# A decoder trunk in fp32: gate and up products of the feed-forward stages by seven quarter products in place of eight

## Chip, core and metric

One core of a Trainium2 chip runs the whole kernel in one launch. The metric is the device time of an execution in microseconds; the profile is one execution of its own, recorded by the hardware profiler. PE is TensorE, DVE is VectorE, ACT is ScalarE, POOL is GpSimd, SP is the engine that issues the loads.

## What is computed

Two layers, each a half-step feed-forward stage, a mixing stage of three kinds of token mixers, and a second half-step feed-forward stage; at the end an RMS norm. There are 512 tokens of width 1024, and the feed-forward width is 2816. The change touches the four feed-forward stages alone:

```python
def rms_norm(x, w):
    xf = x.astype(jnp.float32)
    y = xf * lax.rsqrt(jnp.mean(xf * xf, axis=-1, keepdims=True) + NORM_EPS)
    return (y * w.astype(jnp.float32)).astype(x.dtype)

def swiglu_ffn(h, wg, wu, wd):
    return (jax.nn.silu(h @ wg) * (h @ wu)) @ wd

for l in range(DEPTH):
    h = rms_norm(x, ffn1_norm[l])
    x = x + 0.5 * swiglu_ffn(h, ffn1_w_gate[l], ffn1_w_up[l], ffn1_w_down[l])
    ...
    x = x + mixed @ w_out[l]
    h = rms_norm(x, ffn2_norm[l])
    x = x + 0.5 * swiglu_ffn(h, ffn2_w_gate[l], ffn2_w_up[l], ffn2_w_down[l])
return rms_norm(x, final_norm)
```

## The kernel before

Activations lie transposed, features on the 128 partitions and the 512 tokens along the row: x is 8 tiles of 128x512. To hold fp32 accuracy every matrix operand is split into two fp32r tiles, hi (a cast, on ACT) and lo (operand minus hi, on DVE), and a product is three matmuls per 128 rows of depth: hi by xh, hi by xl, lo by xh. `mm3` (L217) issues them.

A feed-forward stage has 22 blocks of 128 features, in GROUPS of 8, 8 and 6. For each block `mm3` makes pg (gate, 24 matmuls of 128 weight columns by 512 tokens) and pu (up, 24 more) in PSUM. `gated` then multiplies pg by rstd (DVE), takes silu (ACT), multiplies by rstd again (POOL, g<-g,rstd), multiplies pu by that (DVE, u), and splits u into ah (ACT) and al (DVE). The norm works this way: the tokens that enter the products, xh and xl, are x times the norm's weight and not yet divided by the root mean square; the row factor rstd is applied to the products. After a group come its down products pd for 8 output blocks, which are added to x on DVE.

A stage starts before rstd is known: `hold` is the number of first blocks whose `gated` waits (2 in the first stage, 1 in the three others). Then `stats_rows` spreads rstd over the partitions (ps_rb, four small matmuls and a copy), and the held blocks are finished.

Weights come by `load`: SP fetches 1 MB (1024 rows by 256 columns, two feature blocks, as 128x8x256) into one of 2 raw buffers. `dense_units` splits each half of it in turn: hi and lo of 128x1024, of which there are W_BUFS = 4 slots each. So a raw buffer is free for the next load when its second half has been cast and subtracted, and a slot is free when the matmuls that read it have ended.

In the second half of the last stage, `end`, tokens are taken 256 at a time, so matmuls there are 256 wide.

The order of instructions on each engine is set by the tile framework's scheduler, which runs a cost model over the program when it is built; the code gives the program order, priorities and the sizes of the pools. Semaphores follow from what each instruction reads and writes.

## Time and profile before

| | |
|---|---|
| three timed runs | 2185.99, 2188.7, 2189.69 us; median 2188.7 |
| the profiled execution's own time | 2192.0 us |
| its span, first to last instruction | 2190.2 us |
| instructions | 31776, of them 13079 matmuls |
| granted clock of TensorE, mean | 0.992 |
| bytes moved | 203.08 MB, mean 93 GB/s |

The span is the time that the profile's rows divide up; about 2 us of the execution lie around it. A row of a group of instructions reads: line and engine, operation, result <- operands by the program's names, partitions x elements of result and operand, number; then busy us and mean ns of one; then the engine's idle time just before them, and what ended most of it. Line L149 is the helper through which DVE, ACT and POOL record every instruction, so groups are told apart by names. A row of the timeline has the start, the length, the engine and the operation, and in brackets the idle time before it and what ended that. A row of the chain has the start and length of a run of instructions that the end waited for.

### The profile page before, as it was taken

Reading aid. Unit: us, or ns where it says so; the run is one execution under the profiler, and the core shown is the slowest. Engines: PE = TensorE matmul, PEld = TensorE weight load, DVE = VectorE, ACT = ScalarE, POOL = GpSimd, SP = SyncE. Lnnn points to the kernel's source line nnn. Section 1 sums busy time; section 2 is a strip of 40 time slices with the busy share of each in tenths; the row PEclk is TensorE's granted clock in tenths of the full one; section 3 lists DMA queues with packets and bytes.
Section 4 is the critical chain, followed back from the end, with each engine's and each line's share of the span. In section 5 each row is a group of like instructions: output and inputs, shape, how many; then the busy total and the mean of one; then the engine's idle time right before and its main releaser. Section 6 shows DMA issues by size and latency. Waiting matters only on the chain.

```text
span 2190.2 us, 31776 instructions
## 1 busy us (share of the span) xinstructions
PE 2154.9 (98%) x13079; PEld 1829.6 (84%) x13079; DVE 1147.9 (52%) x1980; ACT 842.4 (38%) x1319; POOL 500.4 (23%) x466
## 2 busy tenths in 40 slices
PE   8999999998999999999999999999899999999998
PEld 7888888887988788888888888888889888888888
DVE  5544345468497743433543343364866876434335
ACT  5322224555555422222432222254654544222225
POOL 2201013454333210101211010133633412101011
PEclk9999999999999999999999999999999999999999
DMA  4323234221123323232232322242121232323223
GB/s 155 126 78 116 77 106 140 73 78 40 59 60 106 97 97 96 78 115 80 94 116 96 97 97 96 82 148 79 59 59 40 73 103 88 104 94 99 96 87 126
DMA packets 197757, 203.08 MB, mean 93 GB/s; under 512 B 7626, under 2 KB 189292, under 8 KB 197612
## 3 DMA queue, kind: packets, MB, share of 16 engines
q1 hardware_dynamic: 197612, 201.05, 29.0%
q8 instruction: 103, 1.69, 0.3%
q14 instruction: 42, 0.34, 0.0%
HBM read 194.74 MB, written 6.29 MB: 92 GB/s over the span
## 4 chain that ended last, share of the span: by engine, by line
PE 86%; DVE 9%; ACT 2%; issue 1%; POOL 0%; DMA 0%; SPq 0%; DVEq 0%; ACTq 0%; POOLq 0%
PE pd L217 22%; PE pu L217 22%; PE pg L217 22%; PE ps_fm L260 7%; PE ps_tm L260 5%; PE ps_out L260 2%; DVE aw L149 1%; PE ps_scan L265 1%; DVE lo L149 1%; PE ps_ss L265 1%; DVE blk_p L149 1%; DVE x L149 1%; PE ps_ao L265 1%; DVE flo L149 1%; PE ps_al L265 0%
## 5 line engine op out<-in xcount | busy, mean ns | idle before, releaser
L149 ACT CAST hi<-raw 128x1024 fp32r<-128x1024 f32 (+2 forms) x369 | 379.2, 1028 | 1094.2 <-PE pg L217 323.0
L149 DVE TENSOR_TENSOR lo<-raw,hi 128x1024 fp32r<-128x1024 f32 (+2 forms) x325 | 390.2, 1201 | 80.9 <-ACT hi L149 68.5
L149 POOL TENSOR_TENSOR g<-g,rstd 128x512 f32<-128x512 f32 x88 | 150.2, 1706 | 1130.2 <-ACT g L146 1130.2
L217 PE MATMUL pd<-ah,hi 128*128 128x512 f32 (+1 forms) x752 | 282.0, 375 | 0.0
L217 PE MATMUL pd<-ah,lo 128*128 128x512 f32 (+1 forms) x752 | 281.6, 375 | 0.0
L217 PE MATMUL pd<-al,hi 128*128 128x512 f32 (+1 forms) x752 | 281.6, 375 | 0.0
L217 PE MATMUL pg<-xl,hi 128*128 128x512 f32 x704 | 275.0, 391 | 1.0 <-DVE xl L149 1.0
L217 PE MATMUL pu<-xh,hi 128*128 128x512 f32 x704 | 274.4, 390 | 0.6 <-ACT hi L149 0.6
L217 PE MATMUL pg<-xh,hi 128*128 128x512 f32 x704 | 274.5, 390 | 0.1
L217 PE MATMUL pg<-xh,lo 128*128 128x512 f32 x704 | 274.2, 389 | 0.0
L217 PE MATMUL pu<-xh,lo 128*128 128x512 f32 x704 | 274.1, 389 | 0.0
L217 PE MATMUL pu<-xl,hi 128*128 128x512 f32 x704 | 273.9, 389 | 0.0
L149 DVE TENSOR_TENSOR u<-pu,g 128x512 f32<-128x512 f32 x88 | 60.9, 692 | 280.7 <-PE pu L217 265.2
L149 DVE SCALAR_TENSOR_TENSOR x<-pd,x 128x512 f32<-128x512 f32 (+1 forms) x104 | 67.4, 649 | 229.3 <-PE pd L217 229.0
L149 DVE TENSOR_TENSOR g<-pg,rstd 128x512 f32<-128x512 f32 x88 | 60.8, 691 | 206.8 <-PE pg L217 206.7
L217 PEld LDWEIGHTS pd<-al,hi 128*128 128x128 f32 x752 | 141.4, 188 | 25.7
L217 PEld LDWEIGHTS pd<-ah,lo 128*128 128x128 f32 x752 | 141.3, 188 | 25.4
L217 PEld LDWEIGHTS pd<-ah,hi 128*128 128x128 f32 x752 | 141.1, 188 | 25.5
L217 PEld LDWEIGHTS pg<-xl,hi 128*128 128x128 f32 x704 | 132.3, 188 | 29.3 <-DVE xl L149 2.1
L217 PEld LDWEIGHTS pg<-xh,hi 128*128 128x128 f32 x704 | 132.5, 188 | 27.8 <-ACT xh L149 0.4
L217 PEld LDWEIGHTS pu<-xh,hi 128*128 128x128 f32 x704 | 132.1, 188 | 28.2 <-ACT hi L149 1.0
L217 PEld LDWEIGHTS pu<-xh,lo 128*128 128x128 f32 x704 | 132.3, 188 | 27.5
(331 smaller groups left out, 3778.5 us busy)
## 6 DMA issues: line engine op xcount, KB each, us to landing
raw<-in_ffn_w_gate_dram SPq DMA_DIRECT2D x43, 1024.0 KB, 5.1
raw<-in_ffn_w_up_dram SPq DMA_DIRECT2D x43, 1024.0 KB, 5.1
raw<-in_ffn_w_down_dram SPq DMA_DIRECT2D x32, 1024.0 KB, 4.7
raw<-in_w_in_dram SPq DMA_DIRECT2D x20, 1024.0 KB, 5.2
raw<-in_w_in_dram SPq DMA_DIRECT2D x32, 512.0 KB, 3.6
raw<-in_ffn_w_down_dram SPq DMA_DIRECT2D x20, 768.0 KB, 4.4
xd<-x SPq DMA_DIRECT2D x16, 256.0 KB, 2.5
raw<-in_w_out_dram SPq DMA_DIRECT2D x16, 256.0 KB, 2.6
```

Of the source, the lines that this page charges most:

```text
L149: return f(*args, **kw)
L217: self.nc.tensor.matmul(ps, a[:, k, :], b, start=n == 0, stop=n == 3 * nk - 1)
L260: self.nc.tensor.matmul(ps, a, b, start=start, stop=stop)
L265: self.nc.tensor.matmul(ps, a, b, start=start, stop=stop)
```

## The change

The gate and up products of 18 of the 22 blocks of each stage are made in pairs of blocks by a form of Strassen's method. A pair has a weight of 1024 by 256 and 512 tokens of depth 1024. The weight is cut into four quarters of 512x128 (two halves of the depth, two blocks), the tokens into four of 512x256 (two halves of the depth, two halves of the tokens). Eight products of quarters become seven, on sums of weight quarters and sums of token quarters.

- GROUPS become 6, 6, 6 and 4 blocks. The first 4 blocks of each stage (PLAIN) are made as before; the other 18 are 9 pairs: one in the first group, three, three and two in the next.
- `tokens_mixed`, once per stage after rstd is known: 8 normalised tiles xn (DVE, with weight and rstd), 16 sums tmix of 128x256 (8 on POOL, 8 on DVE), and hi and lo (bh, bl) of the four kinds of quarters, 28 tiles. It stands in the code behind the first block that isn't held.
- `quarter_units`: for each pair the raw gate and up weights, 8 sums of quarters ws on POOL (128x512 each), and for each of the seven products a hi and a lo slot, in which gate and up have a half each: two ACT casts and two DVE subtractions of 128x512.
- `quarters`: for each product 12 matmuls of 256 tokens (four depth blocks by three) for gate and 12 for up, accumulated in pq_y, pq_x and pq_z. Three products are read out on the way to ACT copies (snap), and sums of PSUM and snap are made on DVE, then silu, the multiplication and the split of u. Since xn is normalised, there is no multiplication by rstd, on DVE or on POOL.
- The split tokens xh, xl move to the general pool m (66 buffers, before 50), and two pads shift the pools' addresses.

```diff
-GROUPS = ((0, 8), (8, 8), (16, 6))
+GROUPS = ((0, 6), (6, 6), (12, 6), (18, 4))
+PLAIN = 4
+ORDER = (1, 2, 6, 5, 7, 3, 4)
-M_BUFS = 50
+M_BUFS = 66
...
+    def tokens_mixed(self, w):
...
+        for j in range(KD // 2):
+            xa, xb = self.t2("xn"), self.t2("xn")
+            for d, t in ((j, xa), (j + KD // 2, xb)):
+                v.scalar_tensor_tensor(t, self.x[d], w[:, d:d + 1], self.rstd, ALU.mult, ALU.mult)
+            ta, tb = self.t2("tmix"), self.t2("tmix")
+            gp.tensor_tensor(ta[:, a], xa[:, b], xa[:, a], ALU.subtract)
+            gp.tensor_tensor(tb[:, a], xb[:, b], xa[:, b], ALU.subtract)
+            v.tensor_tensor(ta[:, b], xb[:, b], ta[:, a], ALU.subtract)
+            v.tensor_tensor(tb[:, b], xb[:, a], ta[:, b], ALU.subtract)
...
+            for t, ps in ((xb, (2, 3)), (ta, (5, 6)), (tb, (7, 4))):
+                h, l = self.t2("bh", F32R), self.t2("bl", F32R)
+                nc.scalar.copy(h, t)
+                v.tensor_tensor(l, t, h.bitcast(F32), ALU.subtract)
...
+    def quarter_units(self, srcs):
...
+            def summed(p):
+                for q in parts:
+                    t = self.t2("ws").rearrange("p (k f) -> p k f", k=hk)
+                    x, y, op = {5: (q[21], q[4], ALU.add), 6: (q.get(5), q[1], ALU.subtract),
+                                7: (q[1], q[21], ALU.subtract), 3: (q[2], q.get(6), ALU.subtract)}[p]
+                    nc.gpsimd.tensor_tensor(t, x, y, op)
+                    q[p] = t
+            for p in (5, 6, 7, 3):
+                summed(p)
+            for p in ORDER:
...
+                for i, q in enumerate(parts):
+                    h, l = (t[:, i * hk:(i + 1) * hk, :] for t in (hi, lo))
+                    nc.scalar.copy(h, q[p])
+                    nc.vector.tensor_tensor(l, q[p], h.bitcast(F32), ALU.subtract)
...
+    def quarters(self, units, xq):
...
+        for p in ORDER:
+            ws = next(units)
+            for i in range(2):
...
+                for k in range(hk):
+                    xh, xl = xq[p][k]
+                    for w, r in ((wh, xh), (wh, xl), (wl, xh)):
+                        nc.tensor.matmul(ps, w[:, k, :], r, start=m == 0 and p in (1, 2, 5), stop=m == 3 * hk - 1 and p in (2, 3, 4),
+                                         skip_group_check=True)
...
+                if p == 1:
...
+                    nc.scalar.copy(s1[i], ps)
+                elif p == 2:
+                    nc.vector.tensor_tensor(c1[:, a], ps, s1[i], ALU.add)
...
+                elif p == 7:
+                    nc.vector.tensor_tensor(c2[:, b], ps, s5[i], ALU.add)
+                elif p == 3:
+                    nc.vector.tensor_tensor(c1[:, b], ps, s16[i], ALU.add)
...
     def ffn(self, wg, wu, wd, layer, norm, meanwhile=None, begun=None):
...
+            plain = 0 if gi else PLAIN
...
-            for f in range(nf):
+            for f in range(plain):
...
+                if f == hold:
+                    xq = self.tokens_mixed(w)
+            units = self.quarter_units([m[:, (f0 + plain) * P:(f0 + nf) * P] for m in (wg, wu)])
+            for f in range(plain, nf, 2):
+                act += self.quarters(units, xq)
```

What this does to POOL's queue, at the second group of the first stage (g is the gate of a block, the number is the buffer, the brackets name the semaphores that an instruction waits for). Before, one multiplication per block:

```order
L149 TENSOR_TENSOR g_1258<-g_1258,rstd_434 128x512 [waits Activation_49]
L149 TENSOR_TENSOR g_1326<-g_1326,rstd_434 128x512 [waits Activation_49]
L149 TENSOR_TENSOR g_1398<-g_1398,rstd_434 128x512 [waits Activation_49]
L149 TENSOR_TENSOR g_1466<-g_1466,rstd_434 128x512 [waits Activation_49]
L149 TENSOR_TENSOR g_1538<-g_1538,rstd_434 128x512 [waits DMAHW3_49,DMAHW2_49,DMAHW4_49,DMAHW1_49,DMAHW5_49,DMAHW0_49,DMAHW7_49,PE_49,Activation_49]
```

Now, the sums ws of the group's second pair; raw_1511 is its gate and raw_1513 its up:

```order
L154 TENSOR_TENSOR ws_1515<-raw_1511 128x512 [waits DMAHW0_49,PE_49]
L154 TENSOR_TENSOR ws_1517<-raw_1513 128x512 [waits DMAHW1_49,PE_49]
L154 TENSOR_TENSOR ws_1519<-ws_1515,raw_1511 128x512 [waits PE_49,Pool_49]
L154 TENSOR_TENSOR ws_1521<-ws_1517,raw_1513 128x512 [waits DVE_49,Pool_49]
L154 TENSOR_TENSOR ws_1523<-raw_1511 128x512 [waits PE_49]
L154 TENSOR_TENSOR ws_1525<-raw_1513 128x512 [waits PE_49]
L154 TENSOR_TENSOR ws_1527<-raw_1511,ws_1519 128x512 [waits PE_49,Pool_49]
L154 TENSOR_TENSOR ws_1529<-raw_1513,ws_1521 128x512 [waits PE_49,Pool_49]
```

Eight sums for two blocks stand where two multiplications stood, and the first ones wait for the loads of the pair itself.

DVE at the same pair, where before a block had g, u, al and two lo:

```order
L149 TENSOR_TENSOR g_1466<-pg_1408,rstd_434 128x512 [waits PE_49]
L149 TENSOR_TENSOR lo_1550<-raw_1477,hi_1549 128x1024 [waits Activation_49]
L149 TENSOR_TENSOR u_1470<-pu_1437,g_1466 128x512 [waits PE_49,Pool_49]
L149 TENSOR_TENSOR lo_1579<-raw_1508,hi_1578 128x1024 [waits Activation_49]
L149 TENSOR_TENSOR al_1473<-u_1470,ah_1472 128x512 [waits DMAHW6_49,Activation_49]
```

Now, from the end of the first pair (buffers 1238 to 1241 and 1499 to 1504 are its gate, up and split) into the second (lo from 1532 on). Slots 1532, 1568, 1602 and 1634 are those of products 1, 2, 6 and 5:

```order
L154 TENSOR_TENSOR u_1240<-pq_z_1385,snap_1296 128x256 [waits PE_49]
L154 TENSOR_TENSOR u_1240<-u_1240,g_1238 128x512 [waits DVE_49,Activation_49]
L154 TENSOR_TENSOR lo_1532<-raw_1513,hi_1531 128x512 [waits DMAHW1_49,Activation_49]
L154 TENSOR_TENSOR lo_1568<-raw_1513,hi_1567 128x512 [waits Activation_49]
L154 TENSOR_TENSOR al_1500<-u_1240,ah_1499 128x512 [waits Activation_49]
L154 TENSOR_TENSOR u_1241<-pq_y_1283,g_1239 128x256 [waits PE_49,Activation_49]
L154 TENSOR_TENSOR u_1241<-u_1241,g_1239 128x256 [waits Activation_49]
L154 TENSOR_TENSOR al_1504<-u_1241,ah_1503 128x512 [waits Activation_49]
L154 TENSOR_TENSOR lo_1602<-ws_1519,hi_1601 128x512 [waits Activation_49]
L154 TENSOR_TENSOR lo_1634<-ws_1515,hi_1633 128x512 [waits Activation_49]
L154 TENSOR_TENSOR lo_1634<-ws_1517,hi_1633 128x512 [waits Activation_49]
L154 TENSOR_TENSOR lo_1602<-ws_1521,hi_1601 128x512 [waits Activation_49]
```

Lo of the second pair's up, of products 1 and 2, stands ahead of the first pair's al, the first pair's last multiplications ahead of the lo of products 6 and 5. Product 5's gate lo (lo_1634<-ws_1515) comes after six more of these. PE has the same place in this order; pq_y, pq_x and pq_z are the second pair's accumulators:

```order
L534 MATMUL pq_x_1587<-bl_587,hi_1567 128x256
L534 MATMUL pq_x_1587<-bh_586,lo_1568 128x256
L534 MATMUL pq_z_1639<-bh_516,hi_1633 128x256 [waits Activation_49]
L534 MATMUL pq_z_1639<-bl_517,hi_1633 128x256
L534 MATMUL pq_z_1654<-bh_516,hi_1633 128x256 [waits Activation_49]
L534 MATMUL pq_z_1654<-bl_517,hi_1633 128x256
L534 MATMUL pq_z_1639<-bh_516,lo_1634 128x256 [waits DVE_49]
L534 MATMUL pq_z_1639<-bh_540,hi_1633 128x256
```

Product 2 (slot 1567, 1568) is followed by four matmuls of product 5 with its hi, and then by the first that reads its lo.

DVE at the start of the second feed-forward stage, behind the two first blocks. Before:

```order
L149 TENSOR_TENSOR g_7027<-pg_6952,rstd_6986 128x512
L149 TENSOR_TENSOR lo_7140<-raw_7069,hi_7139 128x1024 [waits PE_49,Activation_49]
L149 TENSOR_TENSOR u_7031<-pu_6998,g_7027 128x512 [waits Pool_49]
L149 TENSOR_TENSOR al_7034<-u_7031,ah_7033 128x512 [waits Activation_49]
L149 TENSOR_TENSOR g_7099<-pg_7037,rstd_6986 128x512 [waits PE_49]
L149 TENSOR_TENSOR lo_7181<-raw_7178,hi_7180 128x1024 [waits DMAHW2_49,Activation_49]
L149 TENSOR_TENSOR u_7103<-pu_7068,g_7099 128x512 [waits PE_49,Pool_49]
```

Now:

```order
L154 TENSOR_TENSOR u_8349<-pu_8316,g_8345 128x512 [waits Pool_49]
L154 TENSOR_TENSOR al_8352<-u_8349,ah_8351 128x512 [waits Activation_49]
L154 SCALAR_TENSOR_TENSOR xn_8355<-x0_7583,sv_a_951,rstd_8304 128x512
L154 SCALAR_TENSOR_TENSOR xn_8356<-x4_7587,sv_a_951,rstd_8304 128x512
L154 TENSOR_TENSOR lo_8620<-raw_8599,hi_8619 128x512 [waits DMAHW6_49,PE_49,Activation_49]
L154 TENSOR_TENSOR tmix_8359<-xn_8356,tmix_8359 128x256 [waits DVE_49,Pool_49]
L154 TENSOR_TENSOR lo_8620<-raw_8601,hi_8619 128x512 [waits DMAHW7_49,Activation_49]
L154 TENSOR_TENSOR bl_8366<-xn_8355,bh_8365 128x256 [waits Activation_49]
L154 TENSOR_TENSOR tmix_8360<-xn_8356,tmix_8359 128x256 [waits DVE_49]
L154 TENSOR_TENSOR bl_8370<-xn_8356,bh_8369 128x512 [waits Activation_49]
L154 TENSOR_TENSOR bl_8374<-tmix_8359,bh_8373 128x512 [waits Activation_49]
L154 TENSOR_TENSOR bl_8378<-tmix_8360,bh_8377 128x512 [waits Activation_49]
```

The lo and gated chain of the third block no longer follow at once: the mixed tokens stand between them, here the first of four depth pairs (xn of x0 and x4).

## The prediction, made before the changed kernel ran

> **What bounds the kernel now.** I read the page's busy times and its chain first, then the chain's steps in order of time, then the groups by form.

> ```profile
> PE 2154.9 (98%) x13079; PEld 1829.6 (84%) x13079; DVE 1147.9 (52%) x1980; ACT 842.4 (38%) x1319; POOL 500.4 (23%) x466
> PE 86%; DVE 9%; ACT 2%; issue 1%; POOL 0%; DMA 0%; SPq 0%; DVEq 0%; ACTq 0%; POOLq 0%
> ```
> ```profile
> 228.74 5.44 PE pu L217 x24
> 234.18 43.52 PE pd L217 x192
> 381.22 6.65 PE ps_tm L260 x54
> 2170.22 10.60 PE pd L217 x90
> ```

> PE is busy for 98% of the span and is 86% of the chain. The chain's rows (start, length, work, count) show what a matmul costs: 24 of 512 columns take 5.44 us, 226.7 ns each, and 192 in a row take 43.52, the same, so PE waits for nothing. The 90 at the end are 256 columns wide: 117.8 ns each, so half the width costs 52%. In the FFNs a saved matmul is saved time now, and any delay of PE's operands is lost time.

> What feeds PE (busy us, mean ns of one | idle before):

> ```profile
> L149 ACT CAST hi<-raw 128x1024 fp32r<-128x1024 f32 x323 | 340.3, 1054 | 987.1 <-PE pg L217 292.0 <-PE pd L217 278.9 <-PE pu L217 272.0
> L149 DVE TENSOR_TENSOR lo<-raw,hi 128x1024 fp32r<-128x1024 f32 x281 | 347.5, 1237 | 70.4 <-ACT hi L149 58.2 <-PE ps_rb L423 7.8
> L149 POOL TENSOR_TENSOR g<-g,rstd 128x512 f32<-128x512 f32 x88 | 150.2, 1706 | 1130.2 <-ACT g L146 1130.2
> L149 DVE TENSOR_TENSOR al<-u,ah 128x512 fp32r<-128x512 f32 x88 | 60.4, 686 | 6.9 <-ACT ah L149 6.9
> L149 ACT CAST ah<-u 128x512 fp32r<-128x512 f32 x88 | 54.8, 623 | 24.8 <-DVE u L149 23.8
> L149 DVE SCALAR_TENSOR_TENSOR bv<-braw,sv_b,bv 128x512 f32<-128x512 f32 x16 | 12.0, 749 | 10.1 <-POOL bv L149 10.1
> L149 DVE SCALAR_TENSOR_TENSOR x<-pd,x 128x256 f32<-128x256 f32 x16 | 6.6, 420 | 7.5 <-PE pd L217 7.5
> L149 ACT ACTIVATE x<-x,sv_a 128x256 f32<-128x256 f32 x16 | 8.1, 511 | 0.3
> L149 ACT ACTIVATE sq<-x 128x256 f32<-128x256 f32 x14 | 5.8, 413 | 3.7 <-DVE x L149 3.6
> ```
> ```profile
> raw<-in_ffn_w_gate_dram SPq DMA_DIRECT2D x43, 1024.0 KB, 5.1
> raw<-in_ffn_w_up_dram SPq DMA_DIRECT2D x43, 1024.0 KB, 5.1
> ...
> raw<-in_w_in_dram SPq DMA_DIRECT2D x20, 1024.0 KB, 5.2
> raw<-in_w_in_dram SPq DMA_DIRECT2D x32, 512.0 KB, 3.6
> ```

> A load of 1 MB lands 5.1 us after its issue; 512 KB more cost 1.6 us (5.2 against 3.6), so a second load issued 0.7 us behind a first lands about 2 × 1.6 less 0.7 = 2.5 us after it, 7.6 after its own issue.

> The row that decides is POOL's 1706 ns. The timeline shows what it is made of (start, length):

> ```profile
> 60.54 1.23 DVE L149 TENSOR_TENSOR lo<-raw,hi 128x1024 fp32r<-128x1024 f32 x1 [0.36 <-ACT hi L149]
> 61.12 1.80 POOL L149 TENSOR_TENSOR g<-g,rstd 128x512 f32<-128x512 f32 x1 [3.64 <-ACT g L146]
> ```
> ```profile
> 339.07 1.29 POOL L149 TENSOR_TENSOR g<-g,rstd 128x512 f32<-128x512 f32 x1 [9.59 <-ACT g L146]
> ```
> ```profile
> 733.26 2.16 DVE L149 TENSOR_TENSOR lo<-raw,hi 128x1024 fp32r<-128x1024 f32 x1
> 735.34 1.78 DVE L149 SCALAR_TENSOR_TENSOR xl<-x,sv_a,xh 128x512 fp32r<-128x512 f32 x1
> ...
> 738.74 0.68 DVE L149 TENSOR_TENSOR x<-ps_out,x 128x512 f32<-128x512 f32 x1
> 739.34 1.65 DVE L149 SCALAR_TENSOR_TENSOR xl<-x,sv_a,xh 128x512 fp32r<-128x512 f32 x1
> ...
> 742.71 0.74 DVE L149 SCALAR_TENSOR_TENSOR xl<-x,sv_a,xh 128x512 fp32r<-128x512 f32 x1
> ```
> ```profile
> 739.15 1.29 POOL L149 TENSOR_TENSOR acc<-acc,sq 128x512 f32<-128x512 f32 x1 [0.88 <-ACT sq L149]
> ```

> A POOL operation of 128x512 takes 1.29 us alone (339.07). At 61.12 it is ready while DVE's lo runs until 61.77, and ends 1.15 after that: it waited. The other way round, xl at 739.34 ends 0.55 after the POOL operation beside it (740.44), though alone it takes 0.74. So a DVE operation that reads two operands in SBUF and a POOL operation never run together here; where both queue they take turns, and a turn of both is 1.15 + 0.55 = 1.70 us. An operation that reads PSUM, x<-ps_out at 738.74, ran its 0.68 us up to POOL's start; in none of these rows is one slowed, so I let those run beside POOL.

> **The change, part by part.** *PE's gain.* Two blocks of 128 features took 4 × 5.44 = 21.76 us; seven products of 24 matmuls of 256 columns take 168 × 0.1178 = 19.79. Per pair −1.97, and 9 pairs × 4 FFNs = 36 pairs: **−71** us. Down projections stay at 226.7 ns a matmul.

> *What is added per pair.* Lo: 14 × 0.69 in place of 4 × 1.24; hi: 14 × 0.62 in place of 4 × 1.05; six PSUM sums and a PSUM multiplication of 256 columns at about 0.42; a multiplication of 0.69 and two al. Two POOL multiplications become 8 sums of weight quarters. What can't overlap POOL on DVE is 14 × 0.69 + 1.1 + 2 × 0.69 = 12.1 us, POOL has 8 × 1.15 = 9.2: together 21.3 of the 19.8 us that PE needs. So inside a group even a perfect order is 1.5 us short per pair; the real order is worse, for the next pair's sums wait for its loads.

> *Waits inside groups.* Take the second pair B of a group from the start of A. Product 6 of A ends at 8.5 (72 matmuls) and frees a hi/lo slot; A's last quarter is cast and subtracted, so the gate's raw slot is free at 9.9 and the up's at 10.6. Their loads land at 15.0 and 18.2 (10.6 + 7.6). POOL then starts eight sums. Ahead of product 5's gate lo in DVE's queue stand lo of up 1 and 2, al, a multiplication, al, and lo of gate 6: with its own seven turns with POOL, 7 × 1.70, and 0.7 for the first cast and a PSUM multiplication between: 18.2 + 12.6 = 30.8. PE has ended A at 19.8, spends 48 matmuls (5.65) on products 1 and 2 and four more (0.47) before it needs that lo, at 25.9: a wait of 4.9. For pair C the same steps, with the slots free at 37.2, loads landing at 42.4 and 45.6 and six turns (10.2) until 55.8, against PE at 36.0 + 5 products' worth 8.5 beyond: 5.2. Of 9 pairs per FFN, groups hold 1, 3, 3 and 2, so five pairs follow another: 2 × (4.9 + 5.2) + 4.9 = 25.1, and four FFNs give **+100**. Bounds: 0 (the order of turns favours DVE) and 1.6 times as much (each turn at 1.70 plus the 0.42 PSUM sums in between). A group's first pair I cost at nothing: its loads and sums lie under 32.6 us of down projection (6 × 24 × 0.2267), in which DVE does little else. If that cover were gone, each would pay what B pays.

> *Mixed tokens.* Once per FFN DVE makes the normalised tokens and their sums. Per feature pair: 2 × 0.75 (the bv row), three sums and lo of 256 columns at 0.42, and three lo of 0.69: 4.8, and about 1.1 of waiting for POOL's two sums: 5.9, four times, with four weight lo (2.8). In front of it stand the gated chains of the first blocks, 754.52 to 759.26, 4.7 each:

> ```profile
> 754.52 0.68 DVE L149 TENSOR_TENSOR g<-pg,rstd 128x512 f32<-128x512 f32 x1
> ...
> 759.26 0.68 DVE L149 TENSOR_TENSOR g<-pg,rstd 128x512 f32<-128x512 f32 x1
> ```

> In FFNs 2 to 4 two such chains and a lo come first, until 11 us after the broadcast of rstd, so product 2's last tokens are there at 11 + 4 × 5.9 = 35. PE has 4 × 5.44 = 21.8 of plain work before product 2 of the pair, and one 5.44 that stands behind it in its queue. After the tokens DVE owes the chains of two more blocks (2 × 4.7, and 1.3 of turns), and the first pair's weight sums stand behind these blocks' multiplications on POOL: three turns (5.1) and 0.69 later product 5's lo is there, at 35 + 10.7 + 5.8 = 51.4. The other 116 matmuls of the pair (13.7) end it at 65.1. Without waits it would end at 21.8 + 5.44 + 19.8 = 47.0: 18 lost each. In FFN 1 PE has only 3 × 5.44 = 16.3 of plain work left and DVE three chains ahead of the tokens: 5.4 less and 4.7 more, a little of it covered: 26. Together 26 + 3 × 18 = **+80**; bounds 40 (half of DVE's work slips under products 1 and 2) and 110.

> *The clock.*

> ```profile
> 489.22 0.25 PE L265 MATMUL ps_al<-aq,ak 128*32 128x32 f32 x2 [2.13 <-DVE ak L149]
> ```
> ```profile
> core 0: us, PE busy (x) PEld busy (x) DVE busy (x) ACT busy (x) POOL busy (x), PEclk, DMA share, GB/s
> ...
> 490.80:494.10 3.30, 3.30 (x9) 2.52 (x9) 3.16 (x8) 0.83 (x2) 1.64 (x5) 0.50 0.39 135
> ```

> After a PE idle of 2.13 us the granted clock was 0.50 over the next stretch (the column PEclk). Half the clock over 3.3 us loses up to 1.7. There would be 20 waits in groups and 4 at the tokens; part of the slow stretch lies in the wait itself, so I take 1.0 each: **+24**, bounds 0 and 41. [...]

> *Ends.* In the last stage a 256-column output block has 12 matmuls, 1.41 us, under ACT's 0.62 + 0.41 + 0.51 = 1.54: +2 over eight blocks and two halves; DVE at the shorter last groups +3: **+5**.

> Sum: −71 + 100 + 80 + 24 + 5 = +138 against the profiled execution's 2192.0 (span 2190.2 and 1.8 around it). That execution lies 3.3 above the median of 2188.7; on the median's side I say **2327**.

> **Rivals.**
> *DVE does not wait for POOL's queue.* If POOL only takes gaps that DVE leaves, product 5's lo is there by 25.9, group waits go, and the token waits fall by the turns in them to about 40: −71 + 40 + 4 + 5 = −22, 2167. For it: PSUM reads aren't slowed. Against: 61.12, 735.34 and 739.34 show both sides waiting. It decides if the lo stands at most 7.7 us (25.9 − 18.2) after the up's load.
> *Loads don't share.* If the up lands 5.1 after its issue, each group wait is 2.5 less: 20 × 2.5 = 50, 2277. For it: the gate and up rows both have 5.1 as median; against: the 512 KB row.
> *Narrow matmuls run at the mixer's pace.* 54 ps_tm matmuls took 6.65, 123.1 ns: 36 × 168 × 5.3 ns = +32, 2359. The end stage's row is nearest, with the same split operands.
> *The clock at its full price*: +17, 2344.

> **How the numbers follow.** 0.2% of 2188.7, 4.4 us, is about what can be told from no change. Chances: the forecast 0.53; DVE unhindered 0.14, of it 0.11 faster and 0.03 within 4.4 us (token waits of 60 in place of 40 make it level); loads not shared 0.16; narrow matmuls slow 0.09; full clock price 0.08. All but the first rival are slower: 0.86. The forecast's own range is 2290 to 2360. The range leaves out the unhindered case and a tail above of some 0.05: 2245, where loads don't share and token waits are at 50, to 2385, where narrow matmuls are slow and token waits at 105.

> **What would show it.** The new products at 24 per 2.83 us; PE idle in the second and third pair of a group ended by DVE's lo on ws, 4 to 6 us; PE idle at each FFN's first pair ended by DVE's bl or lo; lo of 128x512 well above 0.69 (1.2 and more) and POOL's sums at 1.3 to 1.8; granted clock of 0.5 in stretches of FFN stages. Were PE idle below 40 us in all FFNs, the turns would be wrong; were lo at 0.69 while the waits stand, the loads would be the cause.

## The result, and the profile after

The changed kernel took 2379.5 us (2377.0 to 2381.0 in four runs), before 2189.2 (2186.0 to 2190.6 in four): 1.087 times as long, 95% interval 1.0852 to 1.0889. The forecast was 2327 with a range of 2245 to 2385. Direction and range held; the size was 52 us short. The profiled execution took 2377.0 us, its span 2375.2, so the spans differ by 185.0.

First the page of the kernel after: busy times and the chain's shares by engine.

```profile
PE 2175.2 (92%) x15623; PEld 1953.0 (82%) x15623; DVE 1639.6 (69%) x2712; ACT 1079.7 (45%) x2027; POOL 863.3 (36%) x714
PE 54%; DVE 26%; DMA 7%; ACT 7%; issue 4%; POOL 2%; SPq 0%; POOLq 0%; DVEq 0%; ACTq 0%
```

PE, busy for 98% before, now stands idle for 200 us, and DVE's share of the chain went from 9 to 26%. No engine is full: what changed is when PE's operands are there.

Where the time went, by stage: busy time in stretches that end where a feed-forward stage's last down product or a mixing stage's last product ends. Before, with the header of the columns:

```profile
core 0: us, PE busy (x) PEld busy (x) DVE busy (x) ACT busy (x) POOL busy (x), PEclk, DMA share, GB/s
0.00:375.60 375.60, 370.01 (x1637) 305.08 (x1638) 169.32 (x243) 125.10 (x162) 58.97 (x43) 1.00 0.35 113
375.60:734.30 358.70, 347.93 (x3228) 307.28 (x3227) 251.22 (x577) 192.67 (x366) 144.35 (x166) 0.98 0.23 70
734.30:1096.00 361.70, 361.22 (x1602) 299.11 (x1601) 160.52 (x185) 106.59 (x134) 52.28 (x32) 1.00 0.30 97
```

After, the same three stages and the other three:

```profile
0.00:434.20 434.20, 377.50 (x2285) 338.42 (x2286) 289.72 (x423) 182.18 (x333) 142.80 (x102) 0.93 0.30 93
434.20:801.10 366.90, 350.55 (x3227) 309.23 (x3226) 255.75 (x579) 195.80 (x372) 149.83 (x169) 0.97 0.25 74
801.10:1195.60 394.50, 361.93 (x2250) 326.41 (x2249) 277.37 (x365) 164.08 (x307) 140.97 (x92) 0.96 0.28 89
1195.60:1596.50 400.90, 364.76 (x2250) 330.69 (x2249) 274.36 (x362) 163.78 (x305) 137.71 (x90) 0.94 0.28 88
1596.50:1963.80 367.30, 351.01 (x3228) 310.36 (x3227) 258.07 (x580) 196.00 (x372) 149.34 (x167) 0.96 0.25 75
1963.80:2375.20 411.40, 369.42 (x2393) 337.87 (x2391) 284.29 (x407) 177.91 (x343) 142.66 (x97) 0.95 0.28 90
```

The four feed-forward stages are 58.6, 32.8, 39.9 and 36.3 us longer (before: 375.6, 361.7, 361.0 and 375.1). Each should have lost 9 × 1.97 = 18 us of matmuls, so each gave 50 to 76 us back in waits. The mixing stages, whose code was not touched, are 8.2 and 9.2 longer (358.7 and 358.1 before), which the forecast did not have.

Whom PE waited for, after (total us, times, longest); before, one wait of 0.6 us on a hi is all that stands there of hi and lo, and the largest sum was 7.7:

```profile
PE pq_z L534 <- DVE lo L154: 48.1, 24, 4.8
PE pq_z L534 <- ACT hi L154: 43.8, 16, 4.4
PE pq_x L534 <- ACT bh L154: 15.1, 6, 3.0
PE pq_x L534 <- DVE bl L154: 11.9, 9, 1.7
PE ps_sv L1494 <- DMA rows<-in_hgrn_norm_dram: 10.5, 1, 10.5
...
PE ps_ms L417 <- DVE acc L154: 8.9, 2, 4.5
```

The first two are mostly the first product that needs weight sums (product 5, pq_z); the next two are the mixed tokens; then one wait of the first stage and one at the head of each mixing stage.

One following pair, after: the second pair of the second group, whose predecessor starts on PE at 154.4. SP's loads, then POOL, then DVE, then ACT, and PE's two long gaps:

```profile
164.35 0.37 SPq L199 DMA_DIRECT2D raw<-in_ffn_w_gate_dram  x1
164.95 0.39 SPq L199 DMA_DIRECT2D raw<-in_ffn_w_up_dram  x1
```
```profile
170.26 1.30 POOL L154 TENSOR_TENSOR ws<-raw 128x512 f32<-128x512 f32 x1 [13.89 <-PE pq_z L534]
173.03 1.30 POOL L154 TENSOR_TENSOR ws<-raw 128x512 f32<-128x512 f32 x1 [1.47 <-PE pq_y L534]
174.28 3.45 POOL L154 TENSOR_TENSOR ws<-ws,raw 128x512 f32<-128x512 f32 x2
```
```profile
174.80 3.48 DVE L154 TENSOR_TENSOR lo<-raw,hi 128x512 fp32r<-128x512 f32 x2
178.20 1.78 DVE L154 TENSOR_TENSOR al<-u,ah 128x512 fp32r<-128x512 f32 x1
...
182.98 3.58 DVE L154 TENSOR_TENSOR lo<-ws,hi 128x512 fp32r<-128x512 f32 x4
```
```profile
181.42 0.62 ACT L154 CAST ah<-u 128x512 fp32r<-128x512 f32 x1 [5.30 <-DVE u L154]
181.94 2.17 ACT L154 CAST hi<-ws 128x512 fp32r<-128x512 f32 x4
```
```profile
183.13 0.39 PE L534 MATMUL pq_z<-bh,hi 128*128 128x256 f32 x1 [2.92 <-ACT hi L154]
185.41 0.58 PE L534 MATMUL pq_z<-bh,lo 128*128 128x256 f32 x1 [1.26 <-DVE lo L154]
```

The loads go out at 10.0 and 10.6 after the predecessor's start (forecast 9.9 and 10.6), the sums begin at 15.9 and 18.7 (15.0 and 18.2), two sums take 3.45 us and two subtractions 3.48: 1.7 for a turn of both. Product 5's gate lo is the second of the four from 182.98 on. The matmul that reads it starts at 185.4, 31.0 after the start (forecast of the lo 30.8). One step the forecast did not have: PE waited first, and here longer, for product 5's hi. That cast stands on ACT behind ah, for which ACT was idle 5.3 us until DVE, in its turns, had made u. In all twelve second pairs of a group PE's first long gap ends with ACT's hi (34.8 us of idling in sum); in the eight third pairs the gaps end with DVE's lo.

### The profile page after: what moved, and what is told of

The parts are those of the page before. It is cut to its first block, busy times and chain, and to the rows that moved or that the text cites. A ratio compares the mean times of both kernels' runs of the same rounds, so it can differ in the third digit from the quotient of the medians.

```text
span 2375.2 us, 38939 instructions
## 1 busy us (share of the span) xinstructions
PE 2175.2 (92%) x15623; PEld 1953.0 (82%) x15623; DVE 1639.6 (69%) x2712; ACT 1079.7 (45%) x2027; POOL 863.3 (36%) x714
## 4 chain that ended last, share of the span: by engine, by line
PE 54%; DVE 26%; DMA 7%; ACT 7%; issue 4%; POOL 2%; SPq 0%; POOLq 0%; DVEq 0%; ACTq 0%
PE pd L222 18%; PE pq_y L534 10%; DVE lo L154 9%; PE ps_fm L265 5%; PE pq_z L534 5%; DMA raw<-in_ffn_w_gate_dram 4%; PE ps_tm L265 3%; ACT hi L154 3%; PE ps_out L265 3%; DVE u L154 2%; PE pq_x L534 2%; PE pg L222 2%; DVE aw L154 1%; DVE al L154 1%; DMA raw<-in_ffn_w_up_dram 1%
## 5 line engine op out<-in xcount | busy, mean ns | idle before, releaser
L154 ACT CAST hi<-raw 128x512 fp32r<-128x512 f32 (+3 forms) x473 | 351.6, 770 | 589.5 <-PE pd L222 189.4
L154 DVE TENSOR_TENSOR lo<-raw,hi 128x512 fp32r<-128x512 f32 (+2 forms) x429 | 447.7, 1062 | 135.1 <-ACT hi L154 129.0
L154 POOL TENSOR_TENSOR ws<-raw 128x512 f32<-128x512 f32 x144 | 222.8, 1558 | 726.5 <-DMA raw<-in_ffn_w_gate_dram 559.9
L534 PE MATMUL pq_y<-bh,lo 128*128 128x256 f32 x1152 | 330.4, 287 | 9.0 <-DVE lo L154 8.9
L534 PE MATMUL pq_y<-bh,hi 128*128 128x256 f32 x1152 | 330.3, 287 | 5.9 <-ACT bh L154 5.3
L534 PE MATMUL pq_y<-bl,hi 128*128 128x256 f32 x1152 | 329.3, 286 | 3.3 <-DVE bl L154 3.3
L154 DVE TENSOR_TENSOR lo<-ws,hi 128x512 fp32r<-128x512 f32 x288 | 273.4, 995 | 40.8 <-ACT hi L154 39.7
L534 PEld LDWEIGHTS pq_y<-bh,lo 128*128 128x128 f32 x1152 | 223.3, 194 | 12.5 <-DVE lo L154 12.1
L534 PEld LDWEIGHTS pq_y<-bh,hi 128*128 128x128 f32 x1152 | 224.9, 195 | 8.6 <-ACT bh L154 6.6
L534 PEld LDWEIGHTS pq_y<-bl,hi 128*128 128x128 f32 x1152 | 224.4, 195 | 4.9 <-DVE bl L154 4.3
L154 POOL TENSOR_TENSOR lo<-raw,hi 128x1024 fp32r<-128x1024 f32 (+1 forms) x44 | 108.8, 2472 | 197.2 <-ACT hi L154 194.4
## 6 DMA issues: line engine op xcount, KB each, us to landing
raw<-in_ffn_w_gate_dram SPq DMA_DIRECT2D x43, 1024.0 KB, 5.4
raw<-in_ffn_w_up_dram SPq DMA_DIRECT2D x43, 1024.0 KB, 6.7
raw<-in_w_in_dram SPq DMA_DIRECT2D x20, 1024.0 KB, 5.3
raw<-in_w_in_dram SPq DMA_DIRECT2D x32, 512.0 KB, 3.8
raw<-in_ffn_w_down_dram SPq DMA_DIRECT2D x20, 512.0 KB, 3.5
```

The costliest lines, as they stand in the source:

```text
L154: return f(*args, **kw)
L534: nc.tensor.matmul(ps, w[:, k, :], r, start=m == 0 and p in (1, 2, 5), stop=m == 3 * hk - 1 and p in (2, 3, 4), skip_group_check=True)
```

## The experiments

Times are medians beside runs of the kernel before on the same chip (2189.7, 2191.8 and 2190.9 in the three sets).

**The weight sums left out** (no_sums).

```diff
                 for q in parts:
+                    q[p] = q[{5: 21, 6: 4, 7: 1, 3: 2}[p]]
+                    continue
```

> Leaves out the eight sums of weight quarters per pair: products 5, 6, 7 and 3 read raw quarters instead. DVE's and ACT's work and the loads stay as they are; POOL has nothing to do in the pairs. Turns theory (DVE's subtractions and POOL's sums exclude each other): product 5's lo is there at 18.2 + 7 x 0.69 = 23, before PE needs it at 25.9, so a group of three pairs takes 59.4 to 62 us in place of 73.5, and the slow clock behind its waits goes too: four times (2 x 12.5 + 6) = 124 less, and some 3 us per stage less at the tokens: 2235 to 2260. Rival, late loads (the raw buffers come free too late, whatever POOL does): groups of three stay at 70 or more, time at 2360 or more.

Measured: 2221.1 us, 1.0142 (1.0121 to 1.0164) of before. A group of three pairs, after and without the sums:

```profile
260.90:333.60 72.70, 63.91 (x506) 62.61 (x505) 54.02 (x68) 33.96 (x71) 28.30 (x18) 0.95 0.25 80
```
```profile
235.90:295.20 59.30, 59.30 (x505) 59.30 (x504) 37.91 (x69) 33.73 (x71) 0.00 (x0) 1.00 0.32 100
```
```profile
L154 DVE TENSOR_TENSOR lo<-ws,hi 128x512 fp32r<-128x512 f32 x288 | 273.4, 995 | 40.8 <-ACT hi L154 39.7
```
```profile
L154 DVE TENSOR_TENSOR lo<-raw,hi 128x512 fp32r<-128x512 f32 x546 | 368.0, 709 | 152.6 <-ACT hi L154 148.3 <-PE pq_y L536 3.1
```

59.3 us is 504 matmuls at 117.7 ns: no wait is left, though loads come no earlier (the next pair's gate goes out 9.9 us after the group's start) and DVE makes as many subtractions. With its sums on POOL the subtractions of sums take 995 ns (row of after), with POOL silent all of them 709 (row of this run). So the sums are a necessary part of the waits. Late loads alone, the rival, are out. It ran 14 us below its range: the twelve groups gained 140 us, where I had allowed 124, and the wait before the transposes fell from 10.5 to 4.8.

**The sums on DVE** (sums_dve).

```diff
-                    nc.gpsimd.tensor_tensor(t, x, y, op)
+                    nc.vector.tensor_tensor(t, x, y, op)
```

> The eight sums of weight quarters per pair run on DVE instead of POOL; all results are the same. DVE then has 15.2 + 8 x 0.69 = 20.7 us per pair of 19.8 on PE, but takes no turns. Turns theory: four gate sums are done before the up lands, then 4 x 0.69 + 7 x 0.69 + 0.7 from 18.2 on = 26.5, against 25.9: a wait of 0.6 to 2 per following pair; groups of three 61 to 64 us, time 2260 to 2300. Rival, DVE's own load is what is short (its lane is full): with 5.5 us more on it groups of three get longer than 73.5 and the time is above 2380.

Measured: 2289.9 us, inside 2260 to 2300.

```profile
248.00:311.80 63.80, 61.53 (x506) 59.90 (x505) 46.88 (x85) 33.82 (x70) 0.00 (x0) 1.00 0.29 92
```
```profile
L154 DVE TENSOR_TENSOR lo<-ws,hi 128x512 fp32r<-128x512 f32 x288 | 181.2, 682 | 15.8 <-ACT hi L154 15.3
L154 DVE TENSOR_TENSOR ws<-raw 128x512 f32<-128x512 f32 x144 | 93.8, 685 | 58.1 <-DMA raw<-in_ffn_w_up_dram 31.7 <-DMA raw<-in_ffn_w_gate_dram 26.3
```

DVE took the sums over and yet was busy for less of the group, 46.9 us against 54.0: the sums cost it 0.685 each, while sharing with POOL cost 0.3 per subtraction (995 ns against 682) and made each sum 1.6 us long (1558, 1686 and 1644 ns for the three forms of ws after). 90 us came back by moving work to the busier engine. A pair of both takes 1.7 us (after, two sums 3.45 and two subtractions 3.48), far more than the longer one alone (1.29) and not quite the sum of both (0.69 and 1.29): for most of their length these sums and subtractions do not run side by side here.

**Four raw buffers** (raw4), and **the smaller pool by itself** (m58).

```diff
-M_BUFS = 66
+M_BUFS = 58
...
-            self.wraw = pool("wraw", 2)
+            self.wraw = pool("wraw", 4)
```

> Four raw buffers in place of two (and 58 general buffers in place of 66, to make room): the loads of a pair no longer wait until the pair before has given up its raw weights. Late loads theory (the turns cost only because they start with the loads, 18 us into the pair before): sums go ahead in time, what remains is that turns need 21.3 us per pair of 19.8: groups of three pairs at 62 to 66 us in place of 73.5, time 2270 to 2320. Rival, turns alone: whenever the sums run they displace subtractions that PE waits for: groups of three at 71 or more, time above 2350.

Measured: 2253.5 us, 1.0283 (1.0253 to 1.0312) of before: 17 us better than the best I had allowed.

```profile
240.50:300.60 60.10, 59.82 (x506) 59.57 (x505) 50.16 (x70) 33.87 (x71) 23.79 (x16) 1.00 0.30 94
```

The sums are still on POOL, subtractions still take turns (lo<-ws 1021 ns, 682 in sums_dve), and the group of three has no wait worth a name. So in these groups the turns cost PE something only because they begin with a late load; behind the tokens they can cost it even with early loads, as cover shows below. My bound "21.3 us of turns in 19.8" did not bite: 8 of the 24 sums are made before the group starts, under the down projection (16 stand in this window). For m58 two raw buffers stayed:

> Only the general buffers, 58 in place of 66; two raw buffers as in the changed kernel. It tells what of raw4 is the smaller pool. Theory: in the pairs nothing (groups of three stay at 73.5), in the mixing stages the 5 us each by which raw4's were longer (372 and 375 against 367): 2380 + 10, 2375 to 2400. Rival: the smaller pool itself holds something back or helps in the pairs: below 2360 or above 2410.

Measured: 2395.5 us, in its range; a group of three 72.8, a mixing stage 378.6. The smaller pool helps nothing in the pairs and costs 16 us in all, so the gain of raw4 is the loads' alone and was 140 us or more.

**Where the pairs stand** (plain_first, singles). Both make the four plain blocks a group of their own.

```diff
-GROUPS = ((0, 6), (6, 6), (12, 6), (18, 4))
+GROUPS = ((0, 4), (4, 6), (10, 6), (16, 6))
```

> Groups of 4, 6, 6, 6 blocks in place of 6, 6, 6, 4: the four plain blocks of a stage are a group by themselves, so 21.8 us of down projection stand between them and the first pair; the last group has 6 blocks. Theory (the first pair waits for DVE's work on the mixed tokens, which the down projection would cover): the first pair's losses of 26 and 3 x 18 us fall to 10 in sum (-70); the mixing stages get their 358 us back (-17: it is the short last group that delays the row sums behind it); six pairs per stage follow another instead of five, at 6.9 each (+28): about 2320, 2300 to 2335. Rival, the token wait is only moved behind the next wait (the weight sums of the first pair, behind POOL's multiplications): 2360 to 2400.

Measured: 2368.0 us, 33 above its range and inside the rival's. The waits moved, though not to the weight sums that the rival named. PE's waits, word for word, in the first stage up to its first down projection, and in the second stage:

```profile
PE pd L222 <- ACT ah L154: 13.6, 1, 13.6
PE ps_sv L1494 <- DMA rows<-in_hgrn_norm_dram: 7.2, 1, 7.2
```
```profile
PE pu L222 <- DVE g L154: 8.2, 1, 8.2
```

The down projection that was to cover the tokens itself needs the four plain blocks' gated chains, and those stood behind the tokens on DVE. One part did hold: with six blocks in the last group the mixing stages are back at 359.8 and 361.

```profile
426.90:786.70 359.80, 349.14 (x3228) 307.88 (x3226) 249.95 (x576) 192.96 (x365) 145.44 (x166) 0.97 0.22 70
```

In singles nearly every pair is a group:

```diff
-GROUPS = ((0, 6), (6, 6), (12, 6), (18, 4))
+GROUPS = ((0, 4),) + tuple((f, 2) for f in range(4, 18, 2)) + ((18, 4),)
```

> Groups of 4 plain blocks, seven groups of one pair, and a last group of two pairs: nearly every pair has a down projection behind it (10.9 us) in which its successor's loads, sums and subtractions can go on. Theory: DVE and POOL together need 21.3 us plus 5.5 for the additions to x per pair, PE has 30.7, so in-group waits fall from 138 us to four of 6.6 = 26, and token waits to about 10: 2380 - 112 - 71 = 2197, 2180 to 2215. Rival, late loads: the raw buffers come free no earlier, and the small down weights (256 KB) take their places; waits of 5 us and a slow clock behind each remain at most pairs, 36 x 4 = 144: above 2300.

Measured: 2409.4 us, the slowest of all, against 2180 to 2215; the rival is right. SP's queue and POOL's over one pair and its down projection (PE starts the pair at 918.4):

```profile
936.25 8.19 SPq L199 DMA_DIRECT2D raw<-in_ffn_w_down_dram  x4
949.12 0.37 SPq L199 DMA_DIRECT2D raw<-in_ffn_w_gate_dram  x1
950.98 0.37 SPq L199 DMA_DIRECT2D raw<-in_ffn_w_up_dram  x1
```
```profile
929.77 3.45 POOL L154 TENSOR_TENSOR ws<-raw,ws 128x512 f32<-128x512 f32 x2
954.54 1.27 POOL L154 TENSOR_TENSOR ws<-raw 128x512 f32<-128x512 f32 x1 [21.31 <-DMA raw<-in_ffn_w_gate_dram]
```

The down weights pass through the same two raw buffers and wait there for slots; the next gate goes out at 949.1, 4.8 us before the down projection ends, and the first sum that reads it starts at 954.5, after that end. POOL is free for 21 us and has nothing to sum. Time to work in was there; the data was not.

**Fewer mixed tokens** (lean_tokens).

```diff
-            for t, ps in ((xb, (2, 3)), (ta, (5, 6)), (tb, (7, 4))):
+            for t, ps in ((xb, (2, 3)),):
...
+        for p, q in ((5, 2), (6, 3), (7, 2), (4, 3)):
+            out[p] = out[q]
```

> Leaves out the sums of token quarters and their splits: products 4 to 7 read the unmixed second-half tokens. Per stage 16 sums of 256 columns (8 on DVE, 8 on POOL) and 8 hi and 8 lo of 512 columns are gone, on DVE 4 x (2 x 0.42 + 2 x 0.69 + 1.1 of turns) = 13 us. Theory (the first pair waits for DVE's work on the tokens): the loss at the first pair falls from 18.5 to 6 in three stages and from 26 to 14 in the first: 2380 - 50 = 2330, 2315 to 2345. Rival (what the pair waits for is the gated chains and the weight sums behind POOL's multiplications, not the tokens): 2370 or more.

Measured: 2336.7 us, 42.8 below the changed kernel, inside the range. The first pair's loss in the second stage (from the first plain matmul behind the broadcast of rstd to the pair's end, against 47.0 without waits) fell from 18.4 to 9.1. So half of the loss is the work on the mixed tokens; the run takes DVE's, POOL's and ACT's part of it away together and does not tell them apart. What stays is product 5's wait for hi and lo (3.5 and 1.3 us there) and the slow clock behind it.

**All of it away** (bare): no_sums and lean_tokens together, groups of 6, 4, 6, 6, and

```diff
-            if gi == 0 and meanwhile:
+            if gi == 1 and meanwhile:
```

> All suspected costs away at once: no sums of weight quarters, no sums of token quarters and their splits, a last group of six blocks (groups of 6, 4, 6, 6), and the small vectors' loads and transposes one group later. The matmuls are those of the changed kernel. If these four are all that stands beside the saved matmuls, the time is 2189.5 - 71 and what tokens still cost, 4 x 4: about 2135, 2120 to 2160. If something else in the new products costs (narrow matmuls, the PSUM sums, the clock), it is above 2180.

Measured: 2156.9 us, 0.9842 (0.9823 to 0.9862) of before, inside the range. In the second stage

```profile
745.30:1091.50 346.20, 343.95 (x2250) 315.24 (x2249) 216.18 (x352) 162.12 (x303) 19.62 (x13) 1.00 0.31 101
```

346.2 us are 15.5 less than before, of 18 that the matmuls save. The gain of the seven products is real. It is paid for with the sums, and they cost more.

**Versions with the full result** (best, best2, cover). best: sums on DVE, four raw buffers, groups of 6, 4, 6, 6, the small vectors one group later.

> Same results as the changed kernel: weight sums on DVE, four raw buffers (58 general ones), groups of 6, 4, 6, 6 blocks, small vectors one group later. Sums on DVE gave 2290; from there mixing stages -17, the transposes' wait -8, and with the loads early the remaining 6 us per group of three fall to 1 or 2 (DVE needs 20.7 us per pair of 19.8): -40. About 2225, 2205 to 2250; still slower than before by the 75 us that the mixed tokens cost. Rival, early loads don't help DVE since its own queue is in program order: 2260 or more.

Measured: 2272.1 us, against 2205 to 2250: the rival's figure, but its mechanism only in part. Early loads did shorten a group of three with its down projection, from 96.4 us in sums_dve to 95.2 (window 208.8 to 304.0), and the 32.6 of the down projection leave 62.6 where 59.3 would do, in many small waits. What the rest of the 47 us is, this run does not show. best2 is the same with the sums on POOL:

```diff
-                    nc.vector.tensor_tensor(t, x, y, op)
+                    nc.gpsimd.tensor_tensor(t, x, y, op)
```

> Same results as the changed kernel: four raw buffers (58 general ones), weight sums on POOL, groups of 6, 4, 6, 6, the small vectors one group later. From raw4's 2253: mixing stages -17 by the group of six, and the second group of two pairs at no more than 40: about 2236, 2225 to 2250. Rival (the short group as second one brings a wait of its own): 2253 or more.

Measured: 2239.2 us, in its range, 1.0218 (1.0201 to 1.0235) of before; a group of three with its down projection took 92.7. With the loads early, POOL is the better place for the sums. cover: plain_first with four raw buffers, and the tokens behind the plain blocks' chains:

```diff
-                if f == hold:
+                if f == plain - 1:
                     xq = self.tokens_mixed(w)
```

> Same results as the changed kernel: groups of 4, 6, 6, 6 with the four plain blocks by themselves, the mixed tokens behind the chains of all four plain blocks (before them, the down projection waited 8 to 14 us for those chains), four raw buffers (58 general ones). Theory: the first down projection (21.8 us) covers most of DVE's 26 us on the tokens, at the price of one chain of 5 us that it waits for; the first pair's loss falls from 18.5 to about 10. In-group waits stay at nothing as with four buffers alone: 2189.5 - 71 + 4 x 10 + 8 (first stage) + 5 (transposes) + 15 = 2187, 2165 to 2215. Rival, the additions to x and the down weights' subtractions queue behind the tokens on DVE, so the wait only moves into the down projection: 2230 or more.

Measured: 2229.4 us, 1.0176 (1.0161 to 1.0191) of before: the best of these, above its range and at the rival's figure, and still slower than before. The wait moved once more, though not into the down projection, as the rival had it, but into the group behind the tokens (77.0 us, the next one 60.1), where weight sums of two pairs stood in a row:

```profile
828.40:905.40 77.00, 65.76 (x505) 64.11 (x504) 64.63 (x86) 38.19 (x78) 41.69 (x26) 0.91 0.23 73
937.70:997.80 60.10, 59.82 (x506) 59.58 (x505) 50.33 (x71) 34.02 (x72) 23.86 (x16) 1.00 0.30 95
```
```profile
840.36 6.14 DVE L154 TENSOR_TENSOR lo<-ws,hi 128x512 fp32r<-128x512 f32 x4 [3.02 <-ACT hi L154]
...
847.09 6.21 DVE L154 TENSOR_TENSOR lo<-ws,hi 128x512 fp32r<-128x512 f32 x4
853.23 6.84 DVE L154 TENSOR_TENSOR lo<-raw,hi 128x512 fp32r<-128x512 f32 x4
```

Twelve subtractions in 19.2 us, 1.6 each, in step with POOL.

## Why the prediction was right, and where its size was off

*Matmuls, −71.* Right. 168 matmuls take 19.8 us (59.3 a group of three in no_sums), and 256 columns ran at 117.7 ns, not at the mixer's 123, so that rival is out.

*Waits inside groups, +100.* Right in size (gaps between matmuls inside these groups, without slow clock, sum to 104 us in the trace after), mechanism and place: loads out 10 us into the pair, turns of 1.7, product 5's lo read 31.0 us after the start, on PE three gaps of 3.1, 1.4 and 0.3 us, together 4.8 where 4.9 was worked out. That the first of them ends with ACT's hi, not with lo, the forecast did not see; the delay behind both is the same queue of turns on DVE. For the third pair its "36.0 + 8.5" is 44.5, the pair's start on PE; with 6.1 of matmuls more it is the 50.6 that the wait of 5.2 needs. The rival of loads that don't share is out: the page after has 6.7 us from issue to landing for the up and 5.4 for the gate, both 5.1 before. What the steps took for granted is that both halves are needed; the runs show it: without sums no wait (59.3), with early loads no wait (60.1).

*Mixed tokens, +80.* The place was right, the term somewhat large: from the broadcast of rstd to their end the four first pairs lost 28.6, 18.4, 19.0 and 18.8, in sum 85, but with 14 us of slow clock in it; the gaps by themselves are about 70. The working is not as exact as its result: 11 + 4 × 5.9 leaves out the 2.8 of weight lo that it had just named.

*The clock, +24.* This is the term that was mis-sized. In the feed-forward stages of the trace after, the excess of matmul intervals that stand at about twice their length is 51 us in some 480 intervals: 35 us inside groups, 14 at the tokens, 2 behind the transposes; in the kernel before it is 0.5 us in three. About 42 of the 51 us fall where the granted clock is 0.5; the other 9 stand right behind gaps at full clock, where an interval or two take 0.22 us in place of 0.118.

```profile
178.50:181.90 3.40, 1.70 (x15) 1.50 (x13) 2.89 (x3) 0.48 (x1) 3.40 (x3) 1.00 0.00 0
181.90:185.30 3.40, 1.01 (x4) 0.59 (x4) 3.23 (x4) 3.28 (x8) 2.31 (x2) 1.00 0.00 0
185.30:188.70 3.40, 3.29 (x15) 3.29 (x16) 2.52 (x6) 0.75 (x2) 0.00 (x0) 0.50 0.00 0
...
209.20:212.60 3.40, 0.62 (x6) 0.41 (x4) 3.40 (x3) 0.45 (x1) 3.40 (x3) 1.00 0.00 0
212.60:216.00 3.40, 3.06 (x14) 3.06 (x15) 3.40 (x6) 0.52 (x2) 1.42 (x1) 0.50 0.00 0
```

In this trace a stretch at 0.5 does not follow a gap of a certain length, but a stretch of the grid in which PE worked little: 1.01 of 3.40 us ahead of the first, 0.62 ahead of the second, while 1.70 of 3.40 had no consequence. In the feed-forward stages of this trace, from 60 us on, the grid has 411 stretches at full clock. All 25 in which PE was busy for 40% or less were followed by one at 0.5; of the 386 others, which had 47% or more, one was. The row that the forecast went by fits: the 2.13 us of idling were not all, in the 3.4 us ahead of that slow stretch (487.3 to 490.7 before) PE was busy for 1.19. So in this trace where a gap lies on the grid, and whether a second one shares its stretch, decides what it costs, and the tokens, with gap after gap, keep the clock down (0.5 in 23 stretches). In the last row 14 matmuls took 3.06 us, where 14 × 0.1177 are 1.65 at full clock. The first stretch followed gaps of 3.1 and 1.4 us.

*Ends, +5.* Wrong in size: the mixing stages took 17 us more. The short last group leaves DVE 21.9 us instead of 32.8 for the norm's work on x, so the row sums are late: PE waited 4.5 us for acc at the head of each, and slow clock followed. plain_first, with six blocks there, had 359.8 and 361.

*Not in the forecast.* In the first stage PE stood for 10.5 us before transposes of small vectors (ps_sv), whose rows come by DMAs behind the down weights' loads on SP. The third and fourth of those loads wait for raw buffers and go out at 109.5 and 113.0, the rows from 114.0 to 118.2; PE was ready at 108.8. Before, the same DMAs were issued at 95.5 to 99.7, and PE came by at 103. The change moved a step past that queue; I had counted the moved instructions and not this one. Moving it one group further (best2) only moved the wait: 8.1 us there.

So the missing 52 us are: clock 27, mixing stages 12 beyond the 5, transposes 10.5, groups 4, less 10 at the tokens; 5 lie between the profiled executions and the medians, and some 3 in no term named here. That the tokens' term erred the other way and hid 10 us is luck; the group waits, the largest term, came out by their own steps. What stays open is the clock's rule beyond this trace: it was read from one trace, and no run set a gap's length or its place on the grid by itself.

## What to carry over

A saving on the engine that bounds must be set against the engine that feeds it, and against what the feeders share: here 2 us per pair on PE cost six more sums on POOL and ten more subtractions on DVE, which took 1.7 us for one of each where they met. Before blaming the work, ask when its data comes: two more raw buffers took away nearly all of the in-group waits (a group of three 60.1 us in place of 72.7) without a single instruction less. And cover under a long stage is worth nothing if what the stage itself needs stands behind the work that is to be covered.

## What was not expected of the hardware

Moving eight sums from the half-idle POOL to the busier DVE cut DVE's own busy time in a group from 54.0 to 46.9 us. PE's clock fell to 0.5 for 3.4 us at a time, and in the second pairs no gap was that long (3.2 us at most): what preceded it was a stretch of 3.4 us in which PE was busy for 40% or less (25 of 25 in the feed-forward stages after, against 1 of 386 above that). Each such stretch cost about 1 us beside the gaps themselves, 51 us in all with the slow first intervals behind gaps.
